# Tiles of TensorE moved by 32 bytes: a helper tile 32 bytes smaller and three pads of 32 bytes

## Chip, cores and metric

The kernel runs on one core of a Trainium2 chip. The metric is the time of one execution on the device in microseconds (us). Several executions are timed, and one further execution is recorded by the profiler.

## What is computed

One layer of a decoder, on 1024 positions and 1024 channels in float32. A combined projection gives queries, keys, values, two halves of a spatial gating unit, and two gates; two branches are merged; a gated MLP with a causal convolution of width 3 follows.

```python
h = rmsnorm(x, mix_norm)
q, k, v, su, sv, g_a, g_b = split(h @ w_in)
y_att = sliding_window_attention(q, k, v, ...)     # 8 heads, window 128
y_sgu = chunked_spatial_gating(su, sv, ...)        # chunks of 128
x = x + (sigmoid(g_a) * (y_att @ w_oa) + sigmoid(g_b) * (y_sgu @ w_ob)) @ w_out
z = rmsnorm(x, ffn_norm) @ w_up                    # 1024 -> 2 x 2816
x = x + (silu(conv_g(z)) * conv_v(z)) @ w_down
```

## The kernel before

**Arithmetic.** Matrices are multiplied in the float32r type of TensorE. To keep the precision, each operand is split into a high part (a copy on ScalarE, `copy_hi`, L75) and a low part (a subtraction on VectorE or GpSimd), and a product is three matmuls: high by high, high by low, low by high (`mm3`, L79 to L81; `prod`, L1014; the down projection, L1658). The gates and the MLP go by Strassen-like schemes with seven products of half matrices in place of eight; the sums that these need are made beside, on VectorE and GpSimd.

**Matmul shapes.** A matmul reads a stationary operand, 128 partitions by 128 elements, and streams a moving operand of 128 partitions by 512 elements (2048 bytes in a partition) or, in the attention and the projections of its stage, 256 elements (1024 bytes). The stationary operand is loaded by an instruction of its own (LDWEIGHTS, "PEld" in the profile), and each matmul has one. Transposes are matmuls whose moving operand is the unit matrix `ident`, 128 elements wide.

**Stages.** Until about 30 us: keys and values, while `x` arrives. To about 180 us: attention in 16 steps, software-pipelined, with query and `u` projections (`pq`, `pu`) as fillers for TensorE. To about 230 us: the value half of the gating unit (`pvs`, from the weights `wv` and `wvB`) and its mixing (`pm`). Then the gates (`pz`), the two branch projections (`po`), the output projection (`px`), the MLP's 22 pairs of column blocks (`pz` again) and, from about 990 us, the down projection (`pd`, `pdy`). TensorE's order of instructions is the order of the program text (`manual_schedule`); DMAs are issued from SyncE's queue.

**Where tiles lie.** A tile's address is its byte in each partition. A pool takes its tiles one after another in steps of 32 bytes, and pools stand on each other as they are opened, from the left end or (side "right") from the right end of memory; a closed pool's bytes are used again. The pool `base` begins at byte 1152. Its tiles are `cp` (194 float32, 776 bytes, 800 with rounding) at 1152, `sink_b` (32 bytes) at 1952, `ident` at 1984, `ones` at 2496, `mh05` (16 float32, 64 bytes) at 3008, `rstd_b` at 3072, `rstd` (32 bytes) at 7168, and `msk` (512 bytes) at 7200. So the next pool, `big`, begins at 7712, which is 120 times 64 and 32 more. Every later tile that TensorE reads is a multiple of 512 bytes long, so the 32 bytes stay:

- `big` (7 tiles `Y` and one `U` of 16,384 bytes: `x`, `wq`, `wv`, `wkv`, the `T` and `B` operands of the gates and the MLP, `AX`, and the operands of the down projection) and `wst` (weights: raw, high, low);
- the pools that stand on these later (`s3p`, `sg`, `gp`, `wx`, `ex`, `fp`), and `vhl` in the attention's pool `att`;
- on the right side `kp` (`kTh`, `kTl`), `qp` (`qs`, `qr`) and, in their place later, `zr`, since the right end lies at 229,344, also 32 past a multiple of 64.

Behind `vhl` the pool `att` has three tiles of 32 bytes (`kgq`, `eps_x`, `nsink`), so the pools that stand on `att` (`pa`, and `tm` with the probabilities `c`, `ch`, `cl`, `eh`, `el`) begin at 175,744, a multiple of 64. In `zr` lies first `wvB` and then, in the same place, the operand `T3` of the gates, at 212,960. Counted in pairs of 64-byte pieces (128 bytes), the tiles of `big`, `wst` and the pools on them start in the first half of a pair (32 past a multiple of 128), and `kTh`, `qs`, `wvB` and this `T3` in the second (96 past one).

`mh05` is a tile of the constant -0.5, the exponent with which GpSimd takes reciprocal square roots (`rsqrt_cols`, L113); at most 8 of its columns are read.

Of the kernel before, what the change touches and what calls it, by code (L numbers as in the profile page):

```python
# [10 lines left out]
F = mybir.dt.float32  # L11
# [23 lines left out]
def build(tc, a):  # L35
    nc = tc.nc
    ctx = ExitStack()
    with ctx, tc.manual_schedule(engines={mybir.EngineType.PE}):
        body(ctx, tc, nc, a)


def body(ctx, tc, nc, a):
    L, H = slice(0, 512), slice(512, 1024)
    base = ctx.enter_context(tc.tile_pool(name="base", bufs=1))
# [9 lines left out]
    def Y(s, dt=R, shape=None):  # L54
        return big.tile(shape or [128, 4, 1024], dt, tag="Y", name=nm(s), bufs=7)
# [35 lines left out]
    def wsplit(r, s, nk=8):  # L91

        h = wst.tile([128, 8, 128], R, tag="wh", name=nm(s + "h"))
        l = wst.tile([128, 8, 128], R, tag="wl", name=nm(s + "l"))
        copy_hi(h[:, :nk, :], r[:, :nk, :])
        nc.gpsimd.tensor_tensor(l[:, :nk, :], r[:, :nk, :], h[:, :nk, :].bitcast(F), op=ALU.subtract)  # L96
        return h, l
# [3 lines left out]
    sink_b = base.tile([128, 8], F, name="sink_b")  # L101
    ident = base.tile([128, 128], F, name="ident")
    ones = base.tile([128, 128], F, name="ones")
    mh05 = base.tile([128, 16], F, name="mh05")
    rstd_b = base.tile([128, 1024], F, name="rstd_b")
    rstd = base.tile([128, 8], F, name="rstd")
    nc.gpsimd.memset(ones, 1.0)
    nc.gpsimd.memset(mh05, -0.5)
# [11 lines left out]
    def rms_rows(pb, col, hs=(0, 1)):  # L120
# [6 lines left out]
        for h, p in zip(hs, pb):  # L127
# [10 lines left out]
    at = att.__enter__()  # L138
    vhl = at.tile([128, 8, 2, 128], R, name="vhl")
    kgq = at.tile([128, 1], F, name="kgq")  # L140
    eps_x = at.tile([128, 8], F, name="eps_x")
    nsink = at.tile([128, 8], F, name="nsink")
    kp_cm = tc.tile_pool(name="kp", bufs=1, side="right")
    kp = kp_cm.__enter__()
    kTh = kp.tile([128, 2, 1024], R, name="kTh")
    kTl = kp.tile([128, 2, 1024], R, name="kTl")
    ali = kp.tile([128, 8, 128], F, name="ali")
    nc.gpsimd.affine_select(out=ali[:, 0:4, :], in_=ones.unsqueeze(1).to_broadcast([128, 4, 128]),
                            pattern=[[0, 4], [1, 128]], compare_op=ALU.is_gt, fill=0.0, base=0,
                            channel_multiplier=-1)  # L150
# [19 lines left out]
    def rsplit(w, r, c):  # L170

        rv = r.rearrange("p (k a) b -> p k (a b)", a=2)
        ks = slice(4 * c, 4 * c + 4)
        copy_hi(w[:, 0, ks, :], rv)
        nc.gpsimd.tensor_tensor(w[:, 1, ks, :], rv, w[:, 0, ks, :].bitcast(F), op=ALU.subtract)
# [383 lines left out]
    wv, zr, zr_cm = [], [], []  # L559
# [6 lines left out]
    def load_ahead(i):  # L566
        if i < len(items):
            raws[items[i]] = wload(srcs[items[i]], items[i])
# [4 lines left out]
    def weights(n):  # L573

        for i, x in enumerate(items):
            if WHEN.get(x) != n:
                continue
            if x == "q0":
                wq.append(Y("wq", R, [128, 2, 8, 256]))
            if x == "v0":  # L580
                wv.append(Y("wv", R, [128, 2, 8, 256]))
            if x == "z0":
                qp_cm.__exit__(None, None, None)
                kp_cm.__exit__(None, None, None)
                zr_cm.append(tc.tile_pool(name="zr", bufs=1, side="right"))
                zr.append(zr_cm[0].__enter__())
                wv.append(zr[0].tile([128, 2, 8, 256], R, tag="Z", name="wvB"))
            if x[0] == "u":
                ust[("w", int(x[1]))] = wsplit(raws[x], "wu")
            elif x[0] == "q":  # L590
                rsplit(wq[1], raws[x], int(x[1]))
            elif x[0] == "v":
                rsplit(wv[0], raws[x], int(x[1]))
            elif x[0] == "z":
                rsplit(wv[1], raws[x], int(x[1]))
            load_ahead(i + 3)
# [33 lines left out]
    for n in range(20):  # L630
# [18 lines left out]
        if 0 <= n - 2 < 16:  # L649
            p_split(n - 2)  # L650
        weights(n)
        if n == 15:
            rows_again(0)
# [1178 lines left out]
```

## Time and profile before

| | us |
|---|---|
| median of 3 executions | 1195.57 (1195.47 to 1196.32) |
| profiled execution | 1196.68 |
| its span, first to last instruction | 1195.0 |
| TensorE busy in the span | 1183.7 (99%) |
| VectorE busy | 879.7 (74%) |

PE is TensorE's matmul, PEld its weight load, DVE is VectorE, ACT ScalarE, POOL GpSimd, SP SyncE. L1014 is line 1014 of the kernel. In the lists of groups, `pz<-T,qh` is an instruction that writes `pz` and reads `T` (moving) and `qh` (stationary), with buffer numbers left out. The duration of a matmul in the profile runs from its start until its last result is out, and the next matmul starts well before that; what a matmul takes from TensorE is the step from its start to the next one's start, and it is read from the timeline, or from the length of an unbroken run over its count.

### The profile page before, as it was taken

The numbers are of one execution on the slowest core, as the hardware profiler recorded it, in microseconds if no ns is written. First come the engines' busy times: TensorE is split into PE (matmuls) and PEld (weight loads), VectorE is DVE, ScalarE is ACT, GpSimd is POOL, SyncE is SP. The second block draws the span as 40 slices with busy tenths as digits, with TensorE's granted clock in tenths as the row PEclk, the third lists the DMA queues.
The fourth block names the chain that finished last, engine by engine and source line by source line (L and its number), as shares of the span: only waits on it lengthen the run. The fifth ranks groups of instructions, "written<-read, shape, count | busy, mean of one in ns | idle before, by whom it ended". The sixth has DMA issues, their size and how long they took to land.

```text
span 1195.0 us, 15884 instructions
## 1 busy us (share of the span) xinstructions
PE 1183.7 (99%) x5890; PEld 1003.3 (84%) x5890; DVE 879.7 (74%) x1028; ACT 541.7 (45%) x832; POOL 566.7 (47%) x363
## 2 busy tenths in 40 slices
PE   8999999999999999999999999999999999999998
PEld 8989989988888888888888888888888888888886
DVE  7788975745638565668897788878788798775674
ACT  8555567644335222234544445444444445435331
POOL 2367685488768322344756575656657551000000
PEclk9999999999999999999999999999999999999999
DMA  7110133037685997343143242423333268975571
GB/s 271 35 54 19 54 129 137 3 131 266 231 316 208 353 317 278 135 156 109 53 141 108 104 136 103 147 92 123 110 128 124 88 213 288 368 232 194 151 236 63
DMA packets 79133, 191.27 MB, mean 160 GB/s; under 512 B 8912, under 2 KB 9168, under 8 KB 79056
## 3 DMA queue, kind: packets, MB, share of 16 engines
q1 hardware_dynamic: 79056, 190.26, 45.8%
q8 instruction: 46, 0.75, 0.3%
q14 instruction: 31, 0.25, 0.1%
HBM read 139.63 MB, written 50.59 MB: 159 GB/s over the span
## 4 chain that ended last, share of the span: by engine, by line
PE 87%; DVE 6%; DMA 2%; issue 2%; POOL 1%; ACT 1%; SPq 0%; ACTq 0%; POOLq 0%; DVEq 0%
PE pz L1014 46%; PE pdy L1658 8%; PE pd L1658 7%; PE px L80 2%; PE po L81 2%; PE po L80 2%; PE px L81 2%; PE px L79 2%; PE po L79 2%; PE pvs L79 1%; PE pvs L80 1%; PE pvs L81 1%; PE pq L79 1%; DMA ls<-wup 1%; PE pq L81 1%
## 5 line engine op out<-in xcount | busy, mean ns | idle before, releaser
L1014 PE MATMUL pz<-T,qh 128*128 128x512 f32 x472 | 145.5, 390 | 0.0
L974 POOL TENSOR_TENSOR pl<-lp,ph 128x1024 fp32r<-128x1024 f32 x30 | 72.5, 2418 | 82.7 <-ACT ph L75 82.6
L1014 PE MATMUL pz<-B,ph 128*128 128x512 f32 x352 | 109.1, 391 | 0.0
L1014 PEld LDWEIGHTS pz<-T,qh 128*128 128x128 f32 x472 | 88.4, 188 | 18.5 <-ACT u L865 0.3
L1014 PE MATMUL pz<-T,ql 128*128 128x512 f32 x236 | 91.8, 389 | 0.0
L96 POOL TENSOR_TENSOR wjl<-wj,wjh 128x512 fp32r<-128x512 f32 (+1 forms) x24 | 40.7, 1696 | 95.6 <-ACT wjh L75 95.6
L974 POOL TENSOR_TENSOR ql<-lq,qh 128x1024 fp32r<-128x1024 f32 x30 | 77.0, 2566 | 9.1 <-ACT qh L75 9.1
L1014 PEld LDWEIGHTS pz<-B,ph 128*128 128x128 f32 x352 | 65.3, 188 | 14.9 <-ACT x L1505 1.8
L1030 DVE TENSOR_TENSOR pz<-pz,rstd_b 128x1024 f32<-128x1024 f32 x60 | 73.9, 1232 | 4.2 <-ACT rstd_b L128 2.1
L974 POOL TENSOR_TENSOR s3l<-s,s3h 128x512 fp32r<-128x512 f32 x29 | 38.9, 1342 | 70.5 <-ACT s3h L75 66.4
L1014 PE MATMUL pz<-T,s3h 128*128 128x512 f32 x232 | 71.8, 390 | 0.0
L1014 PE MATMUL pz<-B,pl 128*128 128x512 f32 x176 | 68.5, 389 | 0.0
L1658 PE MATMUL pd<-bh,ah 128*128 128x512 f32 x176 | 68.5, 389 | 0.0
L1658 PE MATMUL pd<-bl,ah 128*128 128x512 f32 x176 | 68.5, 389 | 0.0
L1658 PE MATMUL pd<-bh,al 128*128 128x512 f32 x176 | 68.5, 389 | 0.0
L1014 PE MATMUL pz<-T,AX 128*128 128x512 f32 x264 | 63.4, 389 | 0.0
L1014 PE MATMUL pz<-B,AX 128*128 128x512 f32 x264 | 63.4, 389 | 0.0
L1014 PEld LDWEIGHTS pz<-T,AX 128*128 128x128 f32 x264 | 49.5, 188 | 10.3
L1014 PEld LDWEIGHTS pz<-B,AX 128*128 128x128 f32 x264 | 49.6, 188 | 10.3
L1364 DVE SCALAR_TENSOR_TENSOR tg<-pz,cp,tg 128x1023 f32<-128x1023 f32 (+1 forms) x44 | 56.2, 1278 | 0.8
L1364 DVE SCALAR_TENSOR_TENSOR tv<-pz,cp,tv 128x1023 f32<-128x1023 f32 (+1 forms) x44 | 56.2, 1278 | 0.8
L974 POOL TENSOR_TENSOR AX<-lr,AX 128x1024 fp32r<-128x1024 f32 x22 | 53.7, 2442 | 5.1 <-ACT AX L75 5.1
(341 smaller groups left out, 3518.8 us busy)
## 6 DMA issues: line engine op xcount, KB each, us to landing
ls<-wup SPq DMA_DIRECT2D x22, 512.0 KB, 6.0
sum<-ls SPq DMA_DIRECT2D x22, 512.0 KB, 5.6
lp<-wup SPq DMA_DIRECT2D x22, 512.0 KB, 3.5
ra<-wdown SPq DMA_DIRECT2D x44, 256.0 KB, 4.6
b<-T SPq DMA_DIRECT2D x44, 256.0 KB, 3.8
B<-tv SPq DMA_DIRECT2D x33, 256.0 KB, 2.0
T<-tt SPq DMA_DIRECT2D x33, 256.0 KB, 2.0
b<-B SPq DMA_DIRECT2D x33, 256.0 KB, 3.4
```

The lines of the kernel that those rows point to most:

```text
L79: nc.tensor.matmul(out, wh, mh, start=first, stop=False, **kw)
L80: nc.tensor.matmul(out, wh, ml, start=False, stop=False, **kw)
L81: nc.tensor.matmul(out, wl, mh, start=False, stop=last, **kw)
L96: nc.gpsimd.tensor_tensor(l[:, :nk, :], r[:, :nk, :], h[:, :nk, :].bitcast(F), op=ALU.subtract)
L974: nc.gpsimd.tensor_tensor(l, r, h.bitcast(F), op=ALU.subtract)
L1014: nc.tensor.matmul(o, p[:, k, :], y[:, q, k, :], start=not more and k == 0 and j == 0, stop=k == 3 and j == 2, skip_group_check=True)
L1030: nc.vector.tensor_tensor(z, z, rstd_b, op=ALU.mult)
L1364: nc.vector.scalar_tensor_tensor(t[:, j:], p[:, 0:1024 - j], cw[:, ci, 2 - j:3 - j], t[:, j:], op0=ALU.mult, op1=ALU.add)
L1658: nc.tensor.matmul(o[d], p[:, k - k0, m], q[:, k - k0, :], start=new and k == 0 and j == 0, stop=k == HK - 1 and j == 2, skip_group_check= ...
```

## The change

`mh05` gets 8 columns in place of 16 and stands behind `rstd_b`. The pools `att`, `kp` and `zr` each get one more tile of 8 float32 (32 bytes) that nothing writes or reads.

```diff
     ident = base.tile([128, 128], F, name="ident")
     ones = base.tile([128, 128], F, name="ones")
-    mh05 = base.tile([128, 16], F, name="mh05")
     rstd_b = base.tile([128, 1024], F, name="rstd_b")
+    mh05 = base.tile([128, 8], F, name="mh05")
     rstd = base.tile([128, 8], F, name="rstd")
...
     nsink = at.tile([128, 8], F, name="nsink")
+    at.tile([128, 8], F, name="pad_l")
...
     ali = kp.tile([128, 8, 128], F, name="ali")
+    kp.tile([128, 8], F, name="pad_r")
...
                 wv.append(zr[0].tile([128, 2, 8, 256], R, tag="Z", name="wvB"))
+                zr[0].tile([128, 8], F, name="pad_z")
```

By the sizes, `rstd_b` then stands at 3008 and `big` at 7680, 120 times 64. Everything on the left that stood 32 past a multiple of 64 moves down by 32 bytes. The pad in `att` leaves `pa` and `tm` where they were. The pads on the right move `kTh`, `kTl`, `ali`, `qs`, `qr`, `wvB` and `T3` down by 32 bytes too. So all float32r operands of TensorE stand at multiples of 64; those of the left side at the start of a 128-byte pair, and those of the right side (`kTh`, `qs`, `wvB`, `T3` in `zr`) at its middle, as before relative to each other. The instructions are the same, but for the width of one memset.

## The prediction

> **What bounds the kernel now.** I read the page first, then the busy times by stretch, then the chain of waits, and last the timeline of TensorE, instruction by instruction.
>
> ```profile
> span 1195.0 us, 15884 instructions
> PE 1183.7 (99%) x5890; PEld 1003.3 (84%) x5890; DVE 879.7 (74%) x1028; ACT 541.7 (45%) x832; POOL 566.7 (47%) x363
> PEclk9999999999999999999999999999999999999999
> ```
>
> TensorE is busy for 99% of the span at the full granted clock. Only its own instructions can be shortened, or the few waits between them.
>
> ```profile
> core 0: us, PE busy (x) PEld busy (x) DVE busy (x) ACT busy (x) POOL busy (x), PEclk, DMA share, GB/s
> 0.00:30.00 30.00, 26.82 (x188) 25.74 (x189) 22.82 (x38) 25.08 (x45) 8.08 (x11) 0.94 0.75 271
> 30.00:150.00 120.00, 117.76 (x850) 109.67 (x849) 101.74 (x233) 67.56 (x216) 70.26 (x76) 1.00 0.12 40
> 150.00:300.00 150.00, 149.11 (x923) 133.24 (x922) 92.71 (x128) 88.52 (x147) 105.06 (x77) 1.00 0.39 134
> 300.00:1195.00 895.00, 889.97 (x3934) 734.65 (x3932) 662.45 (x633) 360.57 (x425) 383.33 (x200) 1.00 0.51 177
> 370.00:460.00 90.00, 90.00 (x399) 74.54 (x398) 60.69 (x58) 27.75 (x35) 33.84 (x21) 1.00 0.89 316
> 600.00:960.00 360.00, 360.00 (x1587) 296.98 (x1586) 297.16 (x284) 161.96 (x188) 219.46 (x113) 1.00 0.34 118
> 977.00:995.00 18.00, 18.00 (x81) 14.92 (x80) 16.96 (x16) 11.23 (x12) 9.88 (x4) 1.00 0.58 189
> 995.00:1012.00 17.00, 16.75 (x74) 13.54 (x74) 12.35 (x14) 7.60 (x11) 0.00 (x0) 1.00 0.93 316
> ```
>
> These are the stretches on which the sum rests: from 300 us on, 3934 matmuls fill 895 us, and no other engine is near its limit except in the last two rows (DVE 94% busy, then the DMA engines 93%).
>
> ```profile
> 1.71 6.92 DMA xf<-xw
> ...
> 582.36 395.19 PE pz L1014 x1740
> ...
> 977.57 0.71 DVE pz L1023
> ...
> 1001.69 5.42 DMA ra<-wdown
> ...
> 1010.42 30.23 PE pdy L1658 x132
> 1040.65 29.92 PE pd L1658 x132
> ```
>
> In the chain of waits, 1740 matmuls take 395.19 us without a break, 227.1 ns each, and 132 others 29.92 us, 226.7 ns each. Between 977 and 1010 us the chain leaves TensorE and runs through VectorE and a load.
>
> **What one matmul costs, and what its address does to it.** The change moves addresses alone, so I looked for rows where tiles at different addresses are read by matmuls of one shape. All of the `big` and `wst` tiles start 32 bytes past a multiple of 64.
>
> ```profile
> start us, us, engine line op out<-in xcount [idle before <-releaser]
> 251.00 0.63 PE L1014 MATMUL pz<-T,s3h 128*128 128x512 f32 x2
> ...
> 253.80 0.62 PE L1014 MATMUL pz<-x,ph 128*128 128x512 f32 x2
> ...
> 256.54 0.61 PE L1014 MATMUL pz<-T,qh 128*128 128x512 f32 x2
> ...
> 259.26 0.61 PE L1014 MATMUL pz<-T,qh 128*128 128x512 f32 x2
> ```
>
> ```profile
> 190.03 0.28 PE L81 MATMUL pvs<-wv,x 128*128 128x256 f32 x1
> ...
> 191.11 0.28 PE L81 MATMUL pvs<-wv,x 128*128 128x256 f32 x1
> ```
>
> ```profile
> 216.46 0.28 PE L80 MATMUL pvs<-wvB,x 128*128 128x256 f32 x1
> ...
> 217.14 0.28 PE L80 MATMUL pvs<-wvB,x 128*128 128x256 f32 x1
> ```
>
> From 251.00 to 253.80 us stand 12 matmuls that stream `T3` out of the pool `zr`: 233.3 ns each. From 256.54 to 259.26 stand 12 that stream a `T` of `big`: 226.7 ns. Nine on `wv` (in `big`) take 1.08 us, 120.0 ns each; six on `wvB` (in `zr`, the place of `T3`) take 0.68 us, 113.3 ns. Same shapes, same clock, other addresses.
>
> Now the step between these. 226.7 - 120.0 = 106.7 ns for 256 columns more is 0.4167 ns a column, so 512 columns are 213.3 ns and 256 are 106.7. What is left over is 13.3 ns (226.7 and 120.0), 6.7 (113.3) or 20.0 (233.3): always a multiple of 6.67 ns, the time of 16 columns, and 16 float32 are 64 bytes. TensorE seems to fetch its moving operand in pieces of 64 bytes. A row of 2048 bytes that starts in the middle of a piece touches 33 pieces, not 32; the 34 that it costs are these 33 and one more.
>
> What both operands cost at multiples of 64 only the transposes show (`ident` and the probabilities `c` lie so already):
>
> ```profile
> 65.32 0.60 PE L470 MATMUL pt<-ident,c 128*128 128x128 f32 x4
> ...
> L470 PE MATMUL pt<-ident,c 128*128 128x128 f32 x64 | 9.6, 272 | 0.0
> ```
>
> Four take 0.60 us; less the last one's 0.272 that is 109 ns a step (within the 0.01 us of the view), twice the 53.3 ns of 128 columns plus some 2 ns. They pass at two column times a column, so a lost piece could hide there. Against this stands `pv`, whose moving tile lies at a multiple of 64 and whose stationary `vhl` doesn't:
>
> ```profile
> 85.21 0.28 PE L501 MATMUL pv<-ch,vhl 128*128 128x256 f32 x1
> ...
> 86.15 0.28 PE L79 MATMUL pq<-wq,x 128*128 128x256 f32 x1
> ```
>
> Eight in 0.94 us, 117.5 ns each: 10.8 over the columns, only a little under 13.3. So the moving tile alone doesn't decide it; either the stationary tile's 32 bytes count as well, or alignment does little.
>
> **The change part by part.** The halved `mh05` saves at most its one memset's 0.1 us on GpSimd at the start; the pads are neither written nor read. No instruction, wait or DMA is added, and TensorE's order is written out by hand. `ident`, `ones`, `rstd_b` and the attention's `tm` tiles keep a multiple of 64. What changes is every other operand of TensorE, moving and stationary together, and each pair keeps its distance, since both pools of a pair move by 32 bytes. For the aligned pair I have bounds of the leftover: 0 below (columns alone), 13.3 above (nothing changes), and 20.0 if it goes wrong, as `T3` shows. I take some 2 ns from the transposes, the only aligned pair: 33 pieces become 32, and the last one starts in time for the next matmul's first. That saves 11.5 ns a wide matmul, 11.5 on a 256-wide one at 120.0, and 5 on `wvB`.
>
> ```profile
> L79 PE MATMUL pq<-wq,x 128*128 128x256 f32 x128 | 36.6, 286 | 0.5 <-DVE qs L287 0.4 <-DVE cl L479 0.2
> L79 PE MATMUL pvs<-wv,x 128*128 128x256 f32 x64 | 18.2, 284 | 0.0
> L79 PE MATMUL pvs<-wvB,x 128*128 128x256 f32 x64 | 17.7, 277 | 0.0
> L79 PE MATMUL pu<-x,wuh 128*128 128x512 f32 x48 | 19.5, 407 | 0.0
> ```
>
> - 300 to 1195 us: of 3934, some 3,900 are wide (the rest are norms). 3,900 x 11.5 ns = 44.9 us.
> - 150 to 300: of 923, 192 are `wvB` (three lines of 64), about 350 other 256-wide ones (192 on `wv`, the rest `pv`, `sc` and the mixing), about 360 wide: 1.0 + 4.0 + 4.1 = 9.1 us.
> - 30 to 150: 850, of which 384 are `pq` and about 200 others 256-wide, and 144 are `pu`: 6.7 + 1.7 = 8.4 us. Here TensorE already waits for 2.2 us and DVE is 85% busy in short steps that wait in turn for ACT and GpSimd; I credit half, 4.2.
> - 0 to 30: nothing; the chain waits for `x` (6.92 us) and the DMA engines are 75% busy.
> - Given back: from 370 to 460 the DMA engines stand at 89%, so half of 399 x 11.5 ns, 2.3 us, is taken off; from 977 to 1010 VectorE and the loads of `ra` bound the chain, and 5% of 33 us, 1.7, is taken off.
>
> 44.9 + 9.1 + 4.2 - 2.3 - 1.7 = 54.2 us. The profiled execution took 1196.68 us, 1.68 of it outside its span, and lies 1.1 over the median of 1195.57. 1196.7 - 54.2 = 1142.5, and less 1.1 this is 1141 us for the median. With a leftover of 0 the sum grows by 13.3/11.5 to 62.7 (1132, and 1128 if nothing is given back); if the whole attention stretch and 4 us more of the later ones are lost it is 46 (1150). Own range: 1128 to 1150. The cover is thin but there: from 600 to 960 us, in the MLP, DVE's 297 us in 360 (83%) become 87% of a stretch that is 5% shorter; ACT and GpSimd stay lower.
>
> The Trainium skill, "TensorE: Matmul & The Clock Gate", section Back-to-back issue gap, gives for a warm matmul its columns plus 2.5 ns, 215.8 ns at 512. By that the saving would be 10.9 ns, the sum 51 us and the time 1145; the trace's 226.7 does not follow it.
>
> **The rivals.**
>
> Half of it: aligned rows touch 32 pieces, but the second lost piece stays, because it comes from the weight load that runs beside each matmul and not from the straddle. The timeline has both start together:
>
> ```profile
> 1100.65 0.39 PE L1658 MATMUL pdy<-bl,ah 128*128 128x512 f32 x1
> 1100.65 0.19 PEld L1658 LDWEIGHTS pdy<-bh,al 128*128 128x128 f32 x1
> ```
>
> For it: the leftover of `pv`, and that 113.3 against 120.0 depends on which moving tile meets which stationary one. Against it: nothing in the trace is aligned on both sides and wide. Then 6.67 ns a matmul: 26.0 + 2.4 + 2.3 + 2.5 (half of 4.9), less 2.3 given back, is 30.9 us: 1165 us, with 1158 to 1172 as its range.
>
> It does nothing: the leftover depends only on how the two operands lie to each other, and every pair keeps its distance. For it: `T3` (6.67 more) and `wvB` (6.67 less) both start in the other half of a 128-byte pair than their stationary tiles, all other pairs in the same half. Against it: a leftover of exactly two pieces on an odd count is what a straddle would give. 1195.6 us. The Trainium skill, "SBUF — State Buffer", section Specifications (TRN2), names lines of 16 bytes; 32 is a multiple of 16, so by that rule no tile crosses anything it didn't before, and this rival is its result. The steps of 64 bytes in the trace do not look like lines of 16.
>
> Slower: with both operands at the start of a piece, the moving read and the weight load ask for the same place in the same instant, and each wide matmul pays what the ones on `T3` pay, 233.3 ns. Place: `prod` (L1014) and the down projection (L1658). Price: 6.67 ns x (3,900 + 360) = 28 us, 1224 us. It decides once the step of the wide matmuls is above 226.7 ns. Against it: the 32 bytes that are common to both operands now already let them start alike.
>
> **How the numbers follow.** The full gain 0.45, half of it 0.3, nothing 0.12, slower 0.08; 0.05 for a gain outside both ranges. What a measurement of this kernel can tell from no change is about 0.2%, 2.4 us. The predicted time is the likeliest case's, 1141 us. Its range and that of half the gain together run from 1128 to 1172 us and hold about 0.78 of the chance, a bit over with what falls between. Faster 0.8 (0.45 + 0.3 + 0.05), same 0.12, slower 0.08.
>
> **What would show it.** Right: wide matmuls step by 215 to 216 ns in an unbroken run (1740 in some 375 us in place of 395.19), their duration falls from 389 to about 378 ns, and 256-wide ones step by 108 to 110. Half: 220 and 113.3. Nothing: 226.7 still. `T3` in `zr` should stay the odd one out if distance counts beside alignment. The losses would show as waits of TensorE for VectorE in the attention and for loads at 370 to 460 and at 1000 us. The forecast is wrong if the step falls as said and TensorE's share of the span falls under 97%, or if the step doesn't move.

## The result and the profile after

The change moves the time by nothing that can be measured. The median is 1195.72 us (1194.68 to 1196.25, 14 executions) against 1195.48 us for the kernel before in the same rounds (1194.16 to 1196.32, 14 executions). The ratio is 1.0003, with a 95% interval from 0.9995 to 1.0011. The forecast was 1141 us with a range from 1128 to 1172.

The head of the page of the kernel after, and its largest group of matmuls:

```profile
span 1194.5 us, 15884 instructions
PE 1182.8 (99%) x5890; PEld 1002.5 (84%) x5890; DVE 881.3 (74%) x1028; ACT 541.9 (45%) x832; POOL 567.0 (47%) x363
PEclk9999999999999999999999999999999999999999
L1017 PE MATMUL pz<-T,qh 128*128 128x512 f32 x472 | 145.5, 390 | 0.0
```

TensorE is as busy as it was, at the same clock. (`prod` has moved from L1014 to L1017 and the down projection from L1658 to L1661.) A matmul with a 512-wide moving tile still lasts 390 ns, where the forecast had some 378.

The chain of waits after (start, length, engine, what it writes, line, count):

```profile
581.89 397.92 PE pz L1017 x1752
...
1010.04 30.23 PE pdy L1661 x132
1040.27 29.92 PE pd L1661 x132
```

397.92 us over 1752 are 227.1 ns each, and 29.92 over 132 are 226.7: to a tenth of a nanosecond what they were.

The timeline of TensorE after, at the places shown of before:

```profile
start us, us, engine line op out<-in xcount [idle before <-releaser]
250.97 0.63 PE L1017 MATMUL pz<-T,s3h 128*128 128x512 f32 x2
...
253.77 0.62 PE L1017 MATMUL pz<-x,ph 128*128 128x512 f32 x2
...
256.51 0.61 PE L1017 MATMUL pz<-T,qh 128*128 128x512 f32 x2
...
259.23 0.61 PE L1017 MATMUL pz<-T,qh 128*128 128x512 f32 x2
```

```profile
85.22 0.28 PE L503 MATMUL pv<-ch,vhl 128*128 128x256 f32 x1
...
86.16 0.28 PE L79 MATMUL pq<-wq,x 128*128 128x256 f32 x1
...
190.36 0.28 PE L81 MATMUL pvs<-wv,x 128*128 128x256 f32 x1
...
191.44 0.28 PE L81 MATMUL pvs<-wv,x 128*128 128x256 f32 x1
...
216.66 0.28 PE L79 MATMUL pvs<-wvB,x 128*128 128x256 f32 x1
...
217.34 0.28 PE L79 MATMUL pvs<-wvB,x 128*128 128x256 f32 x1
```

Every step that the prediction read is there again: 12 matmuls in 2.80 us with `T3` in `zr` (233.3 ns each), 12 in 2.72 on a `T` of `big` (226.7), 8 in 0.94 for `pv` (117.5), 9 in 1.08 on `wv` (120.0) and 6 in 0.68 on `wvB` (113.3). `pv` had one aligned operand before and has two now, at the same step. No time was saved and given back elsewhere; the step did not move.

### The profile page after: what moved, and what is told of

It reads as the page before. It is cut to its first block, busy times and chain, and to the rows that moved or that the text cites. A ratio compares the mean times of both kernels' runs of the same rounds, so it can differ in the third digit from the quotient of the medians.

```text
span 1194.5 us, 15884 instructions
## 1 busy us (share of the span) xinstructions
PE 1182.8 (99%) x5890; PEld 1002.5 (84%) x5890; DVE 881.3 (74%) x1028; ACT 541.9 (45%) x832; POOL 567.0 (47%) x363
## 4 chain that ended last, share of the span: by engine, by line
PE 90%; DVE 5%; ACT 2%; issue 1%; POOL 1%; DMA 1%; SPq 0%; POOLq 0%; ACTq 0%; DVEq 0%
PE pz L1017 48%; PE pd L1661 10%; PE pdy L1661 8%; PE px L81 2%; PE px L80 2%; PE po L81 2%; PE po L80 2%; PE po L79 2%; PE px L79 2%; PE pvs L79 1%; PE pvs L81 1%; PE pvs L80 1%; PE pq L79 1%; PE pq L81 1%; PE pq L80 1%
## 5 line engine op out<-in xcount | busy, mean ns | idle before, releaser
L1017 PE MATMUL pz<-T,qh 128*128 128x512 f32 x472 | 145.5, 390 | 0.0
L1017 PE MATMUL pz<-B,ph 128*128 128x512 f32 x352 | 109.2, 391 | 0.0
L1017 PEld LDWEIGHTS pz<-T,qh 128*128 128x128 f32 x472 | 88.4, 188 | 18.6 <-ACT u L868 0.3
L1017 PE MATMUL pz<-T,ql 128*128 128x512 f32 x236 | 91.8, 389 | 0.0
L1017 PEld LDWEIGHTS pz<-B,ph 128*128 128x128 f32 x352 | 65.3, 188 | 15.1 <-ACT x L1508 2.0
L1017 PE MATMUL pz<-T,s3h 128*128 128x512 f32 x232 | 71.7, 390 | 0.0
L1017 PE MATMUL pz<-B,pl 128*128 128x512 f32 x176 | 68.5, 389 | 0.0
L1661 PE MATMUL pd<-bh,ah 128*128 128x512 f32 x176 | 68.5, 389 | 0.0
L1661 PE MATMUL pd<-bl,ah 128*128 128x512 f32 x176 | 68.5, 389 | 0.0
L1661 PE MATMUL pd<-bh,al 128*128 128x512 f32 x176 | 68.5, 389 | 0.0
L1017 PE MATMUL pz<-T,AX 128*128 128x512 f32 x264 | 63.4, 389 | 0.0
L1017 PE MATMUL pz<-B,AX 128*128 128x512 f32 x264 | 63.4, 389 | 0.0
L1017 PEld LDWEIGHTS pz<-T,AX 128*128 128x128 f32 x264 | 49.5, 188 | 10.3
L1017 PEld LDWEIGHTS pz<-B,AX 128*128 128x128 f32 x264 | 49.5, 188 | 10.3
```

Of the source, the lines that this page charges most:

```text
L1017: nc.tensor.matmul(o, p[:, k, :], y[:, q, k, :], start=not more and k == 0 and j == 0, stop=k == 3 and j == 2, skip_group_check=True)
L1661: nc.tensor.matmul(o[d], p[:, k - k0, m], q[:, k - k0, :], start=new and k == 0 and j == 0, stop=k == HK - 1 and j == 2, skip_group_check= ...
```

## The experiments

In three of the runs the kernel's own work is left out: a kernel of TensorE alone issues series of matmuls of one kind, each with its own weight load, on constant tiles. In the name of a series, `m` is the moving and `s` the stationary tile, and the number is the byte of the tile at which it starts; by the sizes in the programs all float32r tiles of a run begin 128 past a multiple of 256, so these numbers give the distance. A series of 36 takes 35 steps and then the last one's duration, so the step is (length - duration) / 35, with 388 to 398 ns for the duration in float32r and 379 in bfloat16; for 48 of 256 columns in float32r it is (length - 0.28) / 47. Steps are given to a tenth of a nanosecond from the recorded starts, of which the timeline shows two decimals, without the first few steps of a series, in which it still settles. Below, *distance* is the address of the stationary tile less that of the moving one, modulo 256.

### TensorE alone: all pairs of starts

```diff
+        for n, count in ((512, 36), (256, 48)):
+            for mo in OFF:
+                for so in OFF:
+                    run(mo, so, n, count)
+            for f in FINE:
+                run(f, 0, n, count)
+                run(0, f, n, count)
...
+                    run(mo, so, n, count, mb, sb, 2)
```

`OFF` is (0, 32, 64, 96) and `FINE` (4, 16, 48). The last line is the bfloat16 series, with starts of 0 and 32.

> The kernel's own work is left out: TensorE alone runs unbroken series of matmuls on constant tiles, each series with a fixed start of the moving tile (m) and of the stationary tile (s), in bytes past a multiple of 128. Theory A (distance): the step depends only on m minus s. Equal starts give 226.7 ns at 512 columns and 120.0 at 256, for 0/0, 32/32, 64/64 and 96/96 alike; starts 64 apart give 233.3 and 113.3. Theory B (place): the 233.3 and 113.3 of the full kernel come from where zr lies, not from the start within 128 bytes; all pairs then give 226.7 and 120.0. Theory C (alignment, the forecast's): 0/0, 0/64, 64/0 and 64/64 step by less than every pair with a 32 or 96 in it. Bfloat16 series are run beside: if the leftover of 13.3 ns belongs to operands of 4 bytes, bfloat16 steps by under 218 ns at 512 columns; if to any matmul with a weight load of its own, it shows the 226.7 too.

The timeline of this kernel, two equal starts among unequal ones, and bfloat16:

```profile
42.75 8.58 PE L42 MATMUL ps<-m000x,s096x 128*128 128x512 f32 x36
51.18 8.56 PE L42 MATMUL ps<-m032x,s000x 128*128 128x512 f32 x36
59.58 8.33 PE L42 MATMUL ps<-m032x,s032x 128*128 128x512 f32 x36
...
101.19 8.33 PE L42 MATMUL ps<-m064x,s064x 128*128 128x512 f32 x36
109.36 8.56 PE L42 MATMUL ps<-m064x,s096x 128*128 128x512 f32 x36
...
326.49 7.94 PE L42 MATMUL ps<-mb000x,sb000x 128*128 128x512 bf16 x36
...
349.81 7.93 PE L42 MATMUL ps<-mb032x,sb032x 128*128 128x512 bf16 x36
```

What the wide matmuls did before is, modulo 128, the series 32/32: 8.33 us, a step of 226.7 ns. What they do after is 0/0: 226.7 again (the timeline merges this series with the opening one, whose first eleven steps are slower). 64/64 has its 8.33 us too. The four pairs of equal starts agree; the twelve unequal ones take 228.9 to 234.3, and starts of 4, 16 or 48 against 0 take 231.7 to 236.6. At 256 columns the equal starts take 120.0 ns; starts 64 apart take 113.3 at 0/64, as expected, but 117.8 at 32/96. So the 13.3 ns that were to be shortened are there with both operands at the start of a 64-byte piece, and also of a 128-byte pair. They go with the type: in bfloat16 the step is 215.8 ns, 2.5 over the columns' 213.3, for equal and unequal starts alike.

### The kernel with a gap of 64, and of 32 bytes, between `big` and `wst`

These take the kernel after and shift the stationary operands of `wst`, and the pools above them, against the moving ones of `big`. The first keeps both operands of every 512-wide matmul at multiples of 64, the second doesn't. (`kTh`, `qs` and the attention's probabilities, whose matmuls are narrower, lie 32 past one in the first, since their pads are dropped.)

```diff
+    ctx.enter_context(tc.tile_pool(name="gapp", bufs=1)).tile([128, 16], F, name="gap")
     wst = ctx.enter_context(tc.tile_pool(name="wst", bufs=2))
...
-    at.tile([128, 8], F, name="pad_l")
...
-    kp.tile([128, 8], F, name="pad_r")
```

> The changed kernel with 64 bytes put between the pools big and wst, and without the pads in att and kp (to make room). Moving tiles of big and stationary tiles of wst then lie in different halves of a 128-byte pair, about 2,540 wide matmuls. AX and the down projection, with both operands in big, are the control. Theory A (distance): those 2,540 step by 233.3 ns, AX and the down projection stay at 226.7, the gates' T3 in zr falls from 233.3 to 226.7; 2,540 x 6.67 = 17 us less 0.6 gives some 1212 us. Theory B (place): nothing moves but what the pads did, 1195.7 us, and T3 in zr keeps 233.3.

```diff
+    ctx.enter_context(tc.tile_pool(name="gapp", bufs=1)).tile([128, 8], F, name="gap")
     wst = ctx.enter_context(tc.tile_pool(name="wst", bufs=2))
...
-    at.tile([128, 8], F, name="pad_l")
```

> The changed kernel with 32 bytes between big and wst, and without the pad in att: moving tiles of big stay at multiples of 64, stationary tiles of wst lie 32 past one, as only the attention's pv matmuls did before (117.5 ns at 256 columns). Theory A (distance): wide matmuls with an operand in each pool get a step of their own, between 220 and 233.3 ns, and the time follows, 2,540 x the difference to 226.7; AX and the down projection stay at 226.7. Theory B (place): 226.7 everywhere and 1195.7 us. Theory C (alignment): the stationary tile's straddle costs a piece, 233.3 ns or so for these, 1212 us.

Gap of 64: 1211.64 us (4 executions) against 1195.18, ratio 1.0137 (1.0122 to 1.0152). Gap of 32: 1211.22 us (4 executions), ratio 1.013 (1.0113 to 1.0147). The timeline and the chain of waits of the kernel with 64 bytes:

```profile
257.40 0.63 PE L1016 MATMUL pz<-T,qh 128*128 128x512 f32 x2
...
260.20 0.63 PE L1016 MATMUL pz<-T,qh 128*128 128x512 f32 x2
```

```profile
591.14 405.30 PE pz L1016 x1752
...
1056.49 29.92 PE pd L1660 x132
```

The 12 matmuls on `T` of `big` that took 2.72 us take 2.80: 226.7 has become 233.3. The down projection, whose two operands both lie in `big`, still has 29.92 us over 132, 226.7. By the tiles' addresses 2592 wide matmuls have one operand on either side of the gap; they step by 233.3 ns on average (without the few steps over 245 ns), against 227.1 for the same ones in the kernel after. 2592 x 6.2 ns is 16.1 us, and 1211.64 - 1195.18 is 16.5. In the kernel with 32 bytes these take 233.3 too. The gap of 32 alone couldn't tell distance from alignment, since both theories gave some 1212 us; the gap of 64 does, with slow pairs whose operands both lie at multiples of 64. So alignment to 64 rather than 32 decides nothing, and distance decides.

Two things were missed. The matmuls that keep distance 0 don't all keep 226.7 ns: those that follow a stretch of slow pairs come back to it only after some matmuls.

```profile
707.35 0.39 PE L1016 MATMUL pz<-B,pl 128*128 128x512 f32 x1
707.58 0.62 PE L1016 MATMUL pz<-T,s3h 128*128 128x512 f32 x2
...
709.66 0.62 PE L1016 MATMUL pz<-T,s3h 128*128 128x512 f32 x2
710.12 0.39 PE L1016 MATMUL pz<-T,s3l 128*128 128x512 f32 x1
710.34 0.63 PE L1016 MATMUL pz<-B,ph 128*128 128x512 f32 x2
```

These 12 have both operands above the gap, so distance 0, and take 2.76 us, 230.0 ns each. In the 43 such places of the trace with the gap of 64, the first ten steps average 226.2 to 235.8 ns by their place in the row, and the eleventh and twelfth average 226.7; the control `AX` has 226.7 with `B` and 229.2 with the `T` that follows slow pairs. The distance gives the step of a settled run. And `T3` in `zr` stayed slow, 232.0 ns in the one and 234.1 in the other, where the gap of 64 was to have brought it to 226.7. Its distance in the first had become 128, which I had counted as none.

### TensorE alone: narrower weights, far tiles, other widths

```diff
+for n, count in ((512, 36), (256, 48)):
+    run(0, n, count, (s[0], 0, 128))
+    for c in (96, 64, 32):
+        run(0, n, count, (w[c], 0, c))
+    for o in (4, 16, 48):
+        run(o, n, count, (s[o], o, 128))
+    run(0, n, count, (far, 0, 128))
+    run(0, n, count, (s[0], 0, 128), (alt, 0, 128))
+    run(0, n, count, (far, 64, 128))
+for n in (384, 448):
+    run(0, n, 36, (s[0], 0, 128))
+    run(0, n, 36, (s[64], 64, 128))
```

> The kernel's own work is left out again: unbroken series of float32r matmuls with equal starts of both operands. What is asked is where the leftover of 13.3 ns (16 columns' time, twice) comes from and whether distances over 128 bytes or starts of 4, 16 and 48 bytes count. Theory A (distance) expects 226.7 ns at 512 columns for 4/4, 16/16, 48/48 and for a stationary tile 124 KB away, and 233 with that far tile 64 bytes off; a straddle that costs a piece would put 4/4, 16/16 and 48/48 above 0/0. Theory D: the leftover is made by the weight load that runs beside, so it shrinks with the stationary tile's columns, 220.0 ns at 64 columns and 216.7 at 32. Theory E: the leftover belongs to streaming 4-byte operands, 226.7 at 128, 96, 64 and 32 columns alike. Two stationary tiles in turn: 226.7 by all. 384 and 448 columns: 160.0 + 13.3 = 173.3 and 186.7 + 13.3 = 200.0 if the leftover is fixed for each matmul.

The timeline (`w064` is a stationary tile of 64 columns; `far` lies, by the sizes in the program, 140 KB from `m000`, not 124 as the expectation has it, first at distance 0, then at 64):

```profile
32.93 8.44 PE L37 MATMUL ps<-m000x,w064x 128*64 128x512 f32 x36
...
49.54 8.72 PE L37 MATMUL ps<-m004x,s004x 128*128 128x512 f32 x36
58.10 8.47 PE L37 MATMUL ps<-m016x,s016x 128*128 128x512 f32 x36
66.41 8.44 PE L37 MATMUL ps<-m048x,s048x 128*128 128x512 f32 x36
74.68 8.34 PE L37 MATMUL ps<-m000x,farx 128*128 128x512 f32 x36
...
91.02 8.56 PE L37 MATMUL ps<-m000x,farx 128*128 128x512 f32 x36
99.42 5.92 PE L37 MATMUL ps<-m000x,s000x 128*128 128x256 f32 x48
...
110.74 5.61 PE L37 MATMUL ps<-m000x,w064x 128*64 128x256 f32 x48
...
168.62 7.59 PE L37 MATMUL ps<-m000x,s000x 128*128 128x448 f32 x36
176.05 7.44 PE L37 MATMUL ps<-m000x,s064x 128*128 128x448 f32 x36
```

A weight load of half the columns makes a 256-wide step shorter (120.0 to 113.3 ns) and a 512-wide one longer (226.7 to 230.0). That is against both a load that costs a fixed piece and one that costs by its columns. How far apart the tiles lie doesn't matter (226.7 at 140 KB), nor does taking two stationary tiles in turn (226.7), but the same far tile at distance 64 takes 233.4. With 384 columns it is 173.3 at distance 0, as expected, and 176.7 at 64. With 448 columns and distance 0 the step is 206.7 ns, 20.0 over the columns, where 200.0 was expected, and distance 64 is the faster there, with 202.3. Starts that are equal but no multiple of 32 cost more: 237.8 ns at 4 bytes, 231.1 at 16, 230.1 at 48. Theory A had 226.7 for these three and missed: starts that are no multiple of 32 count after all.

### `T3` in `zr` at a start modulo 128 equal to its stationary tiles'

```diff
-wv.append(zr[0].tile([128, 2, 8, 256], R, tag="Z", name="wvB"))
+zt = zr[0].tile([128, 4112], R, tag="Z", name="wvB")
+wv.append(zt[:, 16:4112].rearrange("p (j k m) -> p j k m", j=2, k=8))
```

The tile is 64 bytes longer, so `T3`, which takes its place later, lies 64 bytes lower; `wvB` stays where it was.

> The changed kernel, with the tile in zr 64 bytes longer: wvB uses the bytes from 64 on and stays where it was, T3 takes the tile from its start and so lies as its stationary tiles do within 128 bytes. Theory A (distance): the 96 matmuls on this T3 step by 226.7 in place of 233.3 ns, 0.64 us in all, 1195.1 us (less than these rounds can tell from 1195.7, so the step is what is read); wvB stays at 113.3. Theory B (place): still 233.3.

1195.39 us (11 executions) against 1195.42, ratio 1.0 (0.9991 to 1.0009). The timeline:

```profile
250.71 0.62 PE L1018 MATMUL pz<-T,s3h 128*128 128x512 f32 x2
...
253.50 0.39 PE L1018 MATMUL pz<-x,ph 128*128 128x512 f32 x1
```

12 in 2.79 us, 232.5 ns: still slow. (The next expectation writes 233.4 for it; the trace has 232.5.) So 128 bytes is not the period either.

### TensorE alone: distances from 0 to 480

```diff
+for n, count in ((512, 36), (256, 48)):
+    for d in range(0, 512, 32):
+        run(0, d, n, count)
+    for o in (8, 12, 24):
+        run(o, o, n, count)
```

> TensorE alone again, float32r, the moving tile at one start and the stationary tile 0 to 480 bytes further in steps of 32 (modulo 512), then equal starts of 8, 12 and 24 bytes. The T3 of t3_equal lay at distance 128 modulo 256 from its stationary tiles and kept 233.4 ns, so a period of 128 has fallen. Theory A2 (distance modulo 256): 226.7 ns at 512 columns at 0 and 256 alone, 233 at 128 and 384. Theory A5 (modulo 512, or more): 226.7 at 0 alone. Theory B (place) would have 226.7 at 128 and 384 too. Theory G (32 bytes is the step that alignment counts in): 8/8, 12/12 and 24/24 step by more than 226.7 at equal distance, like 4/4 (237.8) and 16/16 (231.1); if starts don't count, they give 226.7. Any distance with less than 226.7 at 512 columns would be a kernel to build; none is expected.

```profile
24.07 8.55 PE L35 MATMUL ps<-m000x,s032x 128*128 128x512 f32 x36
32.46 8.56 PE L35 MATMUL ps<-m000x,s064x 128*128 128x512 f32 x36
...
49.28 8.53 PE L35 MATMUL ps<-m000x,s128x 128*128 128x512 f32 x36
...
66.05 8.40 PE L35 MATMUL ps<-m000x,s192x 128*128 128x512 f32 x36
...
82.68 8.33 PE L35 MATMUL ps<-m000x,s256x 128*128 128x512 f32 x36
...
116.06 8.53 PE L35 MATMUL ps<-m000x,s384x 128*128 128x512 f32 x36
...
132.83 8.40 PE L35 MATMUL ps<-m000x,s448x 128*128 128x512 f32 x36
```

Only 0 and 256 give 8.33 us, 226.7 ns. From 32 to 224 the steps are 233.4, 233.4, 234.3, 232.4, 233.3, 228.9 and 233.3 ns, and from 288 to 480 the same seven return in the same order. In a settled series, and with starts at multiples of 32 bytes, the step of a 512-wide float32r matmul goes by the distance modulo 256. It also gives what `T3` in `zr` took in the kernels: at distance 64 (before and after) 233.4 against 233.3 measured, at 128 (the run before this one) 232.4 against 232.5, at 96 (the gap of 32) 234.3 against 234.1.

Equal starts of 8, 12 and 24 bytes step by 231.1, 228.9 and 233.4 ns, more than 226.7, as theory G had it for starts that are no multiple of 32.

At 256 columns the map is another: distances 0 and 256 have the longest step, 120.0 ns, the others 117.3 to 119.9. It isn't settled by the distance alone: distance 64 gave 113.3 and 117.8 ns in the first run, 117.8 here.

### `T3` in `zr` at a multiple of 256

```diff
-wv.append(zr[0].tile([128, 2, 8, 256], R, tag="Z", name="wvB"))
+zt = zr[0].tile([128, 4144], R, tag="Z", name="wvB")
+wv.append(zt[:, 48:4144].rearrange("p (j k m) -> p j k m", j=2, k=8))
```

> The changed kernel, with the tile in zr 192 bytes longer: wvB uses the bytes from 192 on and stays where it was, T3 takes the tile from its start, a multiple of 256 as its stationary tiles are. Theory A2 (distance modulo 256): the 96 matmuls on this T3 now step by 226.7 ns, 0.64 us in all (less than the rounds can tell, so the step is read). If another place in memory counts beside the distance, they keep about 233.

```profile
250.85 0.62 PE L1018 MATMUL pz<-T,s3h 128*128 128x512 f32 x2
...
253.57 0.62 PE L1018 MATMUL pz<-x,ph 128*128 128x512 f32 x2
```

12 in 2.72 us, 226.7 ns: `T3` is no longer the odd one out. Its 96 matmuls save 96 x 6.67 ns = 0.64 us. The time, 1194.52 us (10 executions) against 1195.10, ratio 0.9995 (0.9986 to 1.0005), cannot tell so little from nothing.

## Why the prediction was wrong

**What bounds the kernel** was right: TensorE's step sets the time. The gaps show it from the other side, where 6.2 ns more on 2592 steps, 16.1 us, came out as 16.5 us of the total, with nothing hidden.

**The step that failed** is the reading of the leftover: "a row of 2048 bytes that starts in the middle of a piece touches 33 pieces, not 32; the 34 that it costs are these 33 and one more". Aligned rows cost the same 34 (64/64 and 0/0 beside 32/32 in the first run). Two facts misled me. The leftovers were multiples of the time of 64 bytes, but a multiple says nothing of a boundary: distances 96 and 192 leave 21.0 and 15.6 ns, which are no such multiples. And the rows that I took to show an effect of alignment, `T3` and `wvB` against `wv` and `T` of `big`, differ in distance; the change leaves that as it was.

**The aligned pair's leftover** of some 2 ns was taken from the transposes, "the only aligned pair". They stepped as before and had nothing to tell of 512-wide products, whose aligned pair leaves 13.3 ns (0/0 and 64/64), not 2. `pv` was the row nearer to the question, 256 wide, with the moving tile at a multiple of 64 and a leftover of 10.8 ns. I had put it down as speaking against me and then gave it no weight in the sum. It steps by 117.5 ns with one operand aligned and with both. It is also the exception to "each pair keeps its distance" and to "all other pairs in the same half": by the addresses its moving tiles `ch`, `cl`, `eh`, `el` stand at 64 modulo 128 and stay, while `vhl` moves, so its distance went from 224 to 192. The series at these two distances both have 117.8 ns at 256 columns, so no difference was to be seen.

**The sum**, 11.5 ns on some 5,300 matmuls and 5 ns on 192, failed with its one price: the saving of a matmul was 0. Its counts hold (3,900, 360 and 144 wide ones, and the program has 4404); what I took off for cover was never put to the test.

**Half of it** needed 220 ns; no series has a 512-wide float32r step under 226.7. **Slower** needed more than 226.7 for two operands at the start of a piece; 64/64 shows 226.7.

**It does nothing**, held at 0.12, came true, and for the reason it named: the leftover depends on how the two operands lie to each other, and both moved by the same 32 bytes. Its detail was off: the two halves of a 128-byte pair are not what counts (`T3` 128 off stays at 232.5 ns), but the distance modulo 256. The wide pairs of `big`, `wst` and the pools on them already had distance 0 before the change, and only `T3` in `zr` did not. The Trainium skill's rule that this rival was set beside ("SBUF — State Buffer", section Specifications (TRN2): lines of 16 bytes) agrees with the outcome, but not with the grain: equal starts at 16 bytes step by 231.1 ns, at 32 by 226.7.

**What stays open.** Why float32r leaves 13.3 ns at the best distance, where bfloat16 leaves 2.5, isn't settled. The runs say that it is not the starts at multiples of 32, not how far apart the tiles lie, and not simply the columns of the weight load. That the moving reads and the weight load's reads meet in the same part of memory at a bad distance is a guess that fits a period in bytes; no run shows the part, nor why a slow stretch is felt for ten matmuls more. For the 256-wide products of the attention, another distance between `wq` or `wv` and `x` might be worth up to 6.7 ns each; it wasn't tried.

## What to carry to other kernels

A float32r matmul with 512 columns steps fastest when its two operands lie at the same address modulo 256 and start at multiples of 32 bytes; a gap of one small tile between the pools of its operands cost this kernel 1.3 to 1.4%. An alignment that moved both operands alike changed nothing here, where both were at multiples of 32 already, so before crediting one, look for two rows of one shape in which a single operand's address differs. A row that speaks against the mechanism and is nearer in shape than the row that speaks for it should set the price.

## What the runs showed of the hardware

- For float32r at 512 columns the settled step repeats with the distance in steps of 256 bytes: 226.7 ns at 0 and 256, 228.9 at 192 and 448, 232.4 to 234.3 elsewhere.
- bfloat16 shows none of it in the four pairs tried: 215.8 ns at 512 columns and 109.2 at 256. The Trainium skill, "TensorE: Matmul & The Clock Gate", section Back-to-back issue gap, gives for the isolated gap at 512 by its formula 215.8, and these series agree with it, though they are streams of weight load and matmul, which the section sets apart from that gap; float32r at its best stays 10.9 ns above.
- Widths differ without a plain order at distance 0: leftovers of 13.3 ns at 256 columns, 13.3 at 384, 20.0 at 448 and 13.3 at 512. At 448 distance 64 is the faster (202.3 against 206.7). A narrower stationary tile gains at 256 columns (113.3 ns with 64 columns) and loses at 512 (230.0).
